# Copying the stacked query and key rows of a differential-attention head with six DMAs in place of twelve

## The chip, the cores and the metric

The kernel runs on one core of one Trainium2 chip. The metric is device time in microseconds (us) of one execution; lower is better. Three runs of the kernel before took 710.76, 712.08 and 713.83 us, so the median is 712.08 us.

## The reference

Two decoder layers for 512 tokens of width 1024. Layer 0 joins a gated MLP (A), a differential attention of 8 heads (B) and a cross-attention to 256 memory tokens (M); layer 1 joins a convolution, a sparse attention and another cross-attention. Each layer ends in an output projection and a residual sum. The change lies in B of layer 0:

```python
def diff_attention(q, k, v, lam):
    ...
        s = jnp.einsum('bhmqd,bhmkd->bhmqk', qi, k).astype(jnp.float32) * scale
        s = jnp.where(kpos[None, :] <= qpos[:, None], s, -jnp.inf)
        p = jax.nn.softmax(s, axis=-1)
        pd = p[:, :, 0] - lam * p[:, :, 1]
        return jnp.einsum('bhqk,bhkd->bhqd', pd.astype(v.dtype), v)
```

Each head has two maps (m = 0 and 1) with queries and keys of 32 numbers. The difference of the two softmaxes is multiplied with the values.

## The kernel before, in words

Numbers are held as a high part and a low part (high = the rounded number, low = what the rounding left), and a product is the sum of three TensorE products: high by high, high by low, low by high (`mm3`, L402 to L404). Weights come from DRAM in units of 128x1024 (`load_unit`, DMA at L384); ScalarE makes the high part (L386) and GpSimd the low part (L389).

`b_qk(c)`, c = 0 to 3, projects the queries and keys of two heads (L872, products at L402 to L404), normalizes and rotates them on VectorE (L879 to L887), transposes them on TensorE (L399) and writes high parts `th` (ScalarE, L376) and low parts `tl` (VectorE, L377). In each, index j = 0 is queries and j = 1 keys; rows are the dimensions, columns the 512 tokens.

`b_stack(c, h)` then puts the three products of a head's scores into one: it copies rows of 32 partitions so that 96 partitions hold, for the queries, high, low, high, and for the keys, high, high, low. One matmul over 96 rows then gives the whole score. The copies are DMAs from SBUF to SBUF, issued by SyncE (SP) at L904: 2 maps x 2 sides x 3 row groups = 12 of 32x512 for each head, 96 for the 8 heads.

`b_attn` (L941) goes through the 8 heads. For each it takes the four blocks of 128 queries from the last to the first: `causal_scores` multiplies (L927) and masks (VectorE, L929), ScalarE takes exponentials (L958), VectorE joins the maps (L959 to L962), TensorE transposes (L399 through `transposed`), ScalarE copies (L938), and TensorE multiplies by the values (L965). After a head's first block, the stack of the next head is asked for (L969), so the copies have the rest of the head to arrive. Only the first stack is asked for right before its use (L943).

The work of B is merged with a list of fillers (L1014 to L1016): the projections `b_qk(2)`, `b_qk(3)`, gates, the rest of A, memory keys and values. Then `m_attn` (L590, scores at L601 and L602, exponentials at L607, values at L586 to L588) is merged with the first part of the output projection (`out_part`, L638; products at L402 to L404).

The order of the instructions on each engine isn't the order of the code. `tile.TileContext(nc, schedule_with_timeline_sim=True)` (L1383) orders them at build time by a simulated timeline and adds the waits. Each engine then runs its own list in order. So a change of some DMAs may move instructions on every engine.

SBUF is handed out in pages by `Arena`: the class "x" has pages of 2048 words, and a request of 1024 words cuts one in two.

Of the kernel before, what the change touches and what calls it, by code (L numbers as in the profile page):

```python
# [24 lines left out]
F32R = mybir.dt.float32r  # L25
# [6 lines left out]
P = 128  # L32
S = 512
# [252 lines left out]
def emit(ctx, tc, nc, D, out):  # L286
# [8 lines left out]
    def SC():  # L295
        return Scope(arenas)
# [9 lines left out]
    dma = nc.sync.dma_start  # L306
    act = A.activation

    def f32(t):
        return t.bitcast(F32)  # L310

    def bc(ap, shape):
        return ap.broadcast_to(list(shape))

    def tok(i):
        return slice(i * P, (i + 1) * P)
# [51 lines left out]
    def rstd(sc, ss, scale, n, eps=EPS, parts=P):  # L368
        v = sc([P, n])[:parts]
        G.tensor_scalar(v, ss, scale, eps, MUL, ADD)  # L370
        r = sc([P, n])[:parts]
        G.tensor_tensor(r, v, mhalf[:parts, :n], ALU.pow)  # L372
        return r

    def split(src, h, l, eng=None):
        act(h, src, AF.Copy)  # L376
        (eng or V).tensor_tensor(l, src, f32(h), SUB)  # L377
# [20 lines left out]
    def tr(o, i, k=P):  # L398
        nc.tensor.transpose(o, i, ident[:k, :k])  # L399
# [45 lines left out]
    def proj_N(hs, units, order, n, loaded=()):  # L445


        order = list(order)
        per = S // n
        groups = [order[a:a + per] for a in range(0, len(order), per)]  # L450
        psc = [SC() for _ in groups]
        ps = [c.ps("d", [P, per, n]) for c in psc]
        k0 = 0
        for m, part in enumerate(units):
            with (loaded[m][0] if m < len(loaded) else SC()) as wsc:
                w = loaded[m][1] if m < len(loaded) else unit_parts(wsc, part, n)
                for a, g in enumerate(groups):
                    for b, i in enumerate(g):
                        for j, (wh, wl) in enumerate(w):
                            k = k0 + j  # L460
                            mm3(ps[a][:, b, :], hs[0][k // 4][:, k % 4, tok(i)], hs[1][k // 4][:, k % 4, tok(i)],
                                wh, wl, k + b == 0, k == KT - 1 and b == len(g) - 1)
                    if k0 + len(w) == KT:
                        for b, i in enumerate(g):
                            yield i, ps[a][:, b, :]
                        psc[a].close()
                k0 += len(w)

    def halves(name):
        i, n = UIDX[name]  # L470
        u = [(KT // n, D["wall"][i + j]) for j in range(n)]
        return [u[:n // 2], u[n // 2:]]
# [393 lines left out]
    bst = {}  # L866

    def b_qk(c):

        tsc = SC()  # L870
        th, tl = tsc([P, 2, S], F32R), tsc([P, 2, S], F32R)
        for i, p in proj_N(h0, halves(f"bqk{c}"), range(NT), 256):  # L872
            with SC() as sc:
                t = sc([P, 2, 4, 32])
                t3 = t.rearrange("p j m d -> p (j m) d")
                tf = t.rearrange("p j m d -> p (j m d)")
                act(tf, p, AF.Square)
                ss = sc([P, 8])
                V.tensor_reduce(ss, t3, AX.X, ADD)  # L879
                r = rstd(sc, ss, 1.0 / 32, 8)  # L880
                p4 = p.rearrange("p (j m d) -> p j m d", j=2, d=32)
                u = sc([P, 2, 4, 8])
                V.tensor_tensor(u, p4[:, :, :, 0:8], bc(bsg[:, i, :, :].unsqueeze(2), [P, 2, 4, 8]), MUL)
                V.tensor_tensor(p4, p4, bc(bcg[:, i, :, :].unsqueeze(2), [P, 2, 4, 32]), MUL)
                V.tensor_tensor(p4[:, :, :, 0:4], p4[:, :, :, 0:4], u[:, :, :, 4:8], ADD)
                V.tensor_tensor(p4[:, :, :, 4:8], p4[:, :, :, 4:8], u[:, :, :, 0:4], ADD)
                V.tensor_tensor(t3, p.rearrange("p (j d) -> p j d", d=32), bc(r.unsqueeze(2), [P, 8, 32]), MUL)  # L887
                pt = sc.ps("t", [P, 2, P])
                for k in range(2):
                    tr(pt[:, k, :], tf[:, k * P:(k + 1) * P])  # L890
                split(pt, th[:, :, tok(i)], tl[:, :, tok(i)])
            yield UT / 2 + 220
        bst[c] = (th, tl, tsc)

    def b_stack(c, h):

        th, tl, tsc = bst[c]
        sc = SC()
        st = sc([96, 4, S], F32R)
        for m in range(2):  # L900
            r0 = 64 * h + 32 * m
            for j, srcs in ((1, (th, th, tl)), (0, (th, tl, th))):
                for r, s in enumerate(srcs):
                    dma(f32(st[32 * r:32 * r + 32, 2 * j + m, :]), f32(s[r0:r0 + 32, j, :]))  # L904
        if h == 1:
            tsc.close()
        return st[:, 0:2, :], st[:, 2:4, :], sc
# [33 lines left out]
    def b_attn(order):  # L941
        heads = [(c, g, h) for c in range(2) for g in range(2) for h in range(2)]
        nxt = b_stack(0, 0)  # L943
        for n, (c, g, h) in enumerate(heads):
            ft = 2 * c + g
# [8 lines left out]
            for a, i in enumerate(order):  # L954
                with SC() as sc:
                    e, nm = causal_scores(sc, i, [[(qs[:, m, tok(i)], ks[:, m, :])] for m in range(2)])
                    for m in range(2):
                        act(e[m], e[m], AF.Exp, bias=nm[:, m:m + 1], scale=-1.0, accum_out=l[:, i, m:m + 1])  # L958
                    V.reciprocal(rl[:, i, :], l[:, i, :])  # L959
                    cf = sc([P, 1])  # L960
                    V.scalar_tensor_tensor(cf, l[:, i, 0:1], nlam, rl[:, i, 1:2], MUL, MUL)
                    V.scalar_tensor_tensor(e[1], e[1], cf, e[0], MUL, ADD)  # L962
                    pe = transposed(sc, e[1], i)
                    for k in range(i + 1):
                        mm(o[:, i, :], pe[:, k, :], bV[k // 2][:, k % 2, hc:hc + 64], start=k == 0, stop=k == i)  # L965
                if a == 0 and n + 1 < len(heads):
                    c2, g2, h2 = heads[n + 1]
                    yield from until(lambda: 2 * c2 + g2 in bst)
                    nxt = b_stack(2 * c2 + g2, h2)  # L969
                yield (i + 1) * 430  # L970
# [39 lines left out]
    for c in range(2):  # L1010
        drain(b_qk(c))
    banks(*P_L0)
    move("w", "x", W_DENSE - W_ATTN)
    fill = seq(b_qk(2), b_qk(3), gates_T(h0, [f"bg{f}" for f in range(4)], [yB[a][:, b, :] for a, b in pair]), a_gates(),  # L1014
               mem_prep(), m_q0(), m_gate0(), call(hsc.close), mem_kv(0), mem_kv(1), call(mem_sc.close))
    drain(merge((b_attn(rev), 1.0), (fill, FILL0)))  # L1016
# [328 lines left out]
    srcs = [(yD[0], 4, 2), (yD[1], 6, 2)]  # L1345
# [47 lines left out]
```

## Time and profile before

| | |
|---|---|
| median of 3 runs | 712.08 us (710.76 to 713.83) |
| the profiled execution, its own time | 711.15 us |
| its span in the trace | 709.4 us |
| mean granted TensorE clock | 0.988 of full |
| TensorE (PE) busy | 668.7 us, 94% of the span |
| VectorE (DVE), ScalarE (ACT), GpSimd (POOL) busy | 495.0, 377.8, 391.0 us |
| chain that ended last | PE 70%, DVE 12%, POOL 7%, ACT 4%, DMA 3%, issue 3%, SPq 0% |
| copies of the stacks | 96 DMAs of 64 KB, issued from 89.2 to 199.5 us |

How to read it: the profiled execution is 0.93 us below the median, and 1.75 us of it lie outside the span. PE busy is the time in which a matmul is under way. PE and the weight loads (PEld) run side by side. PEclk is the granted TensorE clock: 1.00 is the upper of its two levels (2.4 GHz), 0.50 the lower (1.2 GHz). SPq is SyncE's queue, which issues all DMAs of this kernel; the time that it takes to issue one is not counted as busy.

### The profile page before, as it was taken

The page shows a single profiled execution, that of the slowest core. Times are in us where ns is not written, and L with a number is a line of the kernel's source. Part 1 is how long each engine was busy: PE and PEld are TensorE (multiplying, and loading weights), DVE is VectorE, ACT ScalarE, POOL GpSimd, SP SyncE. Part 2 cuts the span into 40 slices and gives each one's busy share as a digit, 9 for nine tenths or more (in the row PEclk, how much of TensorE's full clock was granted, in tenths as well). Part 3 has the DMA queues.
Part 4 walks back from the last instruction along what each step waited for, and adds up shares of the span by engine and source line. Part 5 has one row for each costly group of instructions (what it writes and reads, how often), then busy time and mean ns, then how long its engine had stood idle before and what let it go on. Part 6 is the DMA issues. An engine that isn't in the chain of part 4 may idle for free.

```text
span 709.4 us, 11064 instructions
## 1 busy us (share of the span) xinstructions
PE 668.7 (94%) x3819; PEld 567.5 (80%) x3819; DVE 495.0 (70%) x1204; ACT 377.8 (53%) x846; POOL 391.0 (55%) x414
## 2 busy tenths in 40 slices
PE   4999989999999997799999999989999999999997
PEld 3789989888888875688888888768677888788875
DVE  4606668667666865786274979979777877998773
ACT  5345345556455676563353576632445656675541
POOL 3367877475436767442564779956664523421650
PEclk9999999999999999899999999989999999999999
DMA  8532134464313254222232411104021101120121
GB/s 301 185 118 91 60 90 142 136 177 127 107 56 121 88 197 135 85 66 84 65 105 75 148 63 58 61 0 149 31 89 60 61 30 60 42 79 1 61 75 74
DMA packets 22376, 66.56 MB, mean 94 GB/s; under 512 B 3504, under 2 KB 3760, under 8 KB 22320
## 3 DMA queue, kind: packets, MB, share of 16 engines
q1 hardware_dynamic: 22320, 65.86, 28.6%
q8 instruction: 30, 0.49, 0.3%
q14 instruction: 26, 0.21, 0.1%
HBM read 57.46 MB, written 2.10 MB: 84 GB/s over the span
## 4 chain that ended last, share of the span: by engine, by line
PE 70%; DVE 12%; POOL 7%; ACT 4%; DMA 3%; issue 3%; SPq 0%; POOLq 0%; ACTq 0%; DVEq 0%
PE banks L403 17%; PE banks L404 17%; PE banks L402 17%; PE banks L399 5%; PE banks L927 4%; POOL arena_r L389 4%; DMA arena_f<-in_wall_dram 3%; POOL arena_f L372 3%; DVE arena_r L377 2%; PE banks L1212 2%; PE banks L965 2%; ACT arena_r L386 1%; DVE arena_f L929 1%; PE banks L1182 1%; DVE banks L1261 1%
## 5 line engine op out<-in xcount | busy, mean ns | idle before, releaser
L389 POOL TENSOR_TENSOR arena_r<-arena_f,arena_r 128x512 fp32r<-128x512 f32 (+1 forms) x174 | 227.7, 1334 | 183.5 <-ACT arena_r L386 175.4
L402 PE MATMUL banks<-arena_r 128*128 128x512 f32 (+2 forms) x784 | 291.8, 376 | 5.9 <-ACT arena_r L386 1.9
L403 PE MATMUL banks<-arena_r 128*128 128x512 f32 (+2 forms) x784 | 292.2, 373 | 2.2 <-POOL arena_r L389 1.4
L404 PE MATMUL banks<-arena_r 128*128 128x512 f32 (+2 forms) x784 | 290.7, 373 | 0.0
L402 PEld LDWEIGHTS banks<-arena_r 128*128 128x128 f32 x784 | 150.0, 192 | 31.4 <-ACT arena_r L386 3.2
L403 PEld LDWEIGHTS banks<-arena_r 128*128 128x128 f32 x784 | 150.3, 192 | 26.0 <-POOL arena_r L389 2.7
L404 PEld LDWEIGHTS banks<-arena_r 128*128 128x128 f32 x784 | 149.9, 191 | 22.3 <-DVE arena_r L377 0.3
L386 ACT ACTIVATE arena_r<-arena_f 128x1024 fp32r<-128x1024 f32 (+2 forms) x87 | 91.1, 1049 | 67.2 <-issue 19.7
L399 PE MATMUL banks<-const,arena_f 128*128 128x128 f32 (+1 forms) x507 | 81.9, 279 | 13.9 <-DVE arena_f L417 9.4
L929 DVE CUSTOM_DVE_ANT_0 arena_f<-banks,const 128x512 f32<-128x512 f32 (+3 forms) x128 | 60.4, 484 | 35.0 <-PE banks L927 28.5
L376 ACT ACTIVATE arena_r<-banks 128x512 fp32r<-128x512 f32 (+1 forms) x112 | 57.7, 532 | 46.3 <-PE banks L399 32.7
L377 DVE TENSOR_TENSOR arena_r<-banks,arena_r 128x512 fp32r<-128x512 f32 (+1 forms) x112 | 66.7, 608 | 22.2 <-ACT arena_r L376 21.6
L399 PEld LDWEIGHTS banks<-const,arena_f 128*128 128x128 f32 (+1 forms) x507 | 61.9, 144 | 25.1 <-DVE arena_f L417 9.9
L372 POOL TENSOR_TENSOR arena_f<-arena_f,const 128x4 f32<-128x4 f32 (+3 forms) x60 | 68.0, 1135 | 3.6
L1261 DVE SCALAR_TENSOR_TENSOR banks<-arena_f,const,banks 128x482 f32<-128x482 f32 (+14 forms) x90 | 66.1, 734 | 1.4
L927 PE MATMUL banks<-arena_r 128*128 128x512 f32 (+7 forms) x192 | 50.8, 339 | 4.4 <-DVE arena_f L929 2.1
L958 ACT ACTIVATE arena_f<-arena_f 128x512 f32<-128x512 f32 (+3 forms) x64 | 35.8, 562 | 26.6 <-DVE arena_f L929 26.2
L1189 ACT ACTIVATE arena_f<-arena_f 128x256 f32<-128x256 f32 (+3 forms) x64 | 35.6, 559 | 26.0 <-DVE arena_f L929 25.2
L657 DVE TENSOR_TENSOR arena_f<-arena_f,banks 128x512 f32<-128x512 f32 x40 | 27.0, 684 | 26.6 <-PE banks L404 26.0
L574 POOL TENSOR_SCALAR arena_f<-arena_f 128x512 f32<-128x512 f32 (+3 forms) x32 | 19.9, 626 | 39.6 <-DVE arena_f L1191 33.7
L927 PEld LDWEIGHTS banks<-arena_r 128*128 128x128 f32 (+1 forms) x192 | 32.8, 190 | 10.6 <-DVE arena_f L929 4.6
L1259 POOL TENSOR_TENSOR arena_f<-arena_f 128x482 f32<-128x482 f32 (+29 forms) x30 | 37.8, 1259 | 2.9 <-DVE arena_f L608 0.9
(177 smaller groups left out, 809.8 us busy)
## 6 DMA issues: line engine op xcount, KB each, us to landing
arena_f<-in_wall_dram SPq DMA_DIRECT2D x88, 512.0 KB, 3.3
arena_r<-arena_r SPq DMA_DIRECT2D x96, 64.0 KB, 2.0
arena_f<-in_x_dram SPq DMA_DIRECT2D x7, 512.0 KB, 6.0
arena_f<-in_w_dram SPq DMA_DIRECT2D x4, 512.0 KB, 3.8
out_dram<-arena_f SPq DMA_DIRECT2D x8, 256.0 KB, 2.0
arena_f<-in_norms_dram SPq DMA_DIRECT2D x3, 512.0 KB, 4.3
arena_f<-in_mem_dram SPq DMA_DIRECT2D x2, 512.0 KB, 3.2
arena_f<-in_wqb_dram SPq DMA_DIRECT2D x2, 420.0 KB, 3.2
```

The costliest lines, as they stand in the source:

```text
L372: G.tensor_tensor(r, v, mhalf[:parts, :n], ALU.pow)
L376: act(h, src, AF.Copy)
L377: (eng or V).tensor_tensor(l, src, f32(h), SUB)
L386: act(h, raw, AF.Copy)
L389: G.tensor_tensor(l[:, c], raw[:, c], f32(h[:, c]), SUB)
L399: nc.tensor.transpose(o, i, ident[:k, :k])
L402: mm(o, lh, rh, start=first, stop=False)
L403: mm(o, lh, rl, start=False, stop=False)
L404: mm(o, ll, rh, start=False, stop=last)
L927: mm(t[:, a % per, :], q, k[:, :w], start=b == 0, stop=b == len(qk) - 1)
L929: V.tensor_tensor_reduce(e[a], t[:, a % per, :], cmask[:, S - w:], -1.0, -NEG, ADD, ALU.min, nm[:, a:a + 1])
L1261: V.scalar_tensor_tensor(acc[:, z:], hc[:, :S - z], cw[:, f, k:k + 1], acc[:, z:], MUL, ADD)
```

## The change

High and low parts of queries and keys lie in one tile `tt` of four planes: query high, query low, key high, key low. `th` and `tl` are now views of it with a step of two planes. A copy takes a query plane and a key plane at once: two runs of 512 words for each of 32 partitions, at a step of 2, 1 or 3 planes in the source and 2 in the target. So a head's stack is 2 maps x 3 row groups = 6 DMAs of 32x2x512, 48 for the 8 heads. What is computed, and what is stored in the stack, stay the same.

```diff
     def b_qk(c):
 
         tsc = SC()
-        th, tl = tsc([P, 2, S], F32R), tsc([P, 2, S], F32R)
+        tt = tsc([P, 4, S], F32R)
+        th, tl = tt[:, 0::2, :], tt[:, 1::2, :]
...
-        bst[c] = (th, tl, tsc)
+        bst[c] = (tt, tsc)
 
     def b_stack(c, h):
 
-        th, tl, tsc = bst[c]
+        tt, tsc = bst[c]
         sc = SC()
         st = sc([96, 4, S], F32R)
         for m in range(2):
             r0 = 64 * h + 32 * m
-            for j, srcs in ((1, (th, th, tl)), (0, (th, tl, th))):
-                for r, s in enumerate(srcs):
-                    dma(f32(st[32 * r:32 * r + 32, 2 * j + m, :]), f32(s[r0:r0 + 32, j, :]))
+            for r, (q, k) in enumerate(((0, 2), (1, 2), (0, 3))):
+                dma(f32(st[32 * r:32 * r + 32, m::2, :]), f32(tt[r0:r0 + 32, q:k + 1:k - q, :]))
```

The scheduler's order changes with it. The lines of `b_qk` from L872 on are one higher in the changed file, L904 and what follows keep their numbers. Three places:

The DMA list of SyncE from the first stack on, before (-) and now (+); L904 are the copies of the stacks, L384 the weight units, L839 and L843 two constants of A.

```order
-L904 DMA arena_r<-arena_r 32x512 x24
+L904 DMA arena_r<-arena_r 32x2x512 x12
+L384 DMA arena_f<-in_wall_dram 128x1024 x4
+L904 DMA arena_r<-arena_r 32x2x512 x18
+L384 DMA arena_f<-in_wall_dram 128x1024 x4
+L904 DMA arena_r<-arena_r 32x2x512 x9
+L839 DMA arena_f<-in_wsT_dram 128x512
+L904 DMA arena_r<-arena_r 32x2x512 x3
 L384 DMA arena_f<-in_wall_dram 128x1024 x3
-L904 DMA arena_r<-arena_r 32x512 x36
```

The first two stacks still stand together at the head of the list, and the next three behind one more group of weight loads; four such loads stand between them where there were three.

TensorE at the first head's first scores. L399 x2 are transposes of `b_qk(1)`, L402 to L404 the products of `b_qk(2)`, L927 the scores: 512 columns for the last block of queries, 384 for the one before it. Before:

```order
L404 MATMUL banks<-arena_r 128x256
L399 MATMUL banks<-const,arena_f 128x128 x2
L927 MATMUL banks<-arena_r 128x512
L399 MATMUL banks<-const,arena_f 128x128 x2
L402 MATMUL banks<-arena_r 128x256
L403 MATMUL banks<-arena_r 128x256
```

Now:

```order
L404 MATMUL banks<-arena_r 128x256
L399 MATMUL banks<-const,arena_f 128x128 x2
L927 MATMUL banks<-arena_r 128x512 x2
L927 MATMUL banks<-arena_r 128x384
L399 MATMUL banks<-const,arena_f 128x128 x2
L402 MATMUL banks<-arena_r 128x256
```

The second map's scores of the last block stood 46 products, four more transposes and one 384-column score further down; they now follow the first map's at once, with a score of the next block behind them, ahead of all products of `b_qk(2)`.

TensorE at the start of `m_attn`, before (-) and now (+): L601 and L602 are its scores, L399 x4 the transposes of its exponentials, L402 and L403 products of the output projection.

```order
 L601 MATMUL banks<-arena_r 128x256
 L602 MATMUL banks<-arena_r 128x256
+L399 MATMUL banks<-const,arena_f 128x128 x4
 L601 MATMUL banks<-arena_r 128x256
 L602 MATMUL banks<-arena_r 128x256
 L601 MATMUL banks<-arena_r 128x256
 L602 MATMUL banks<-arena_r 128x256
-L402 MATMUL banks<-arena_r 128x512
-L403 MATMUL banks<-arena_r 128x512
```

Twelve products of the output projection stood behind the scores; four transposes now stand among the scores, and the products come later. So the cross-attention runs further ahead of the output projection: behind its last product with the values (L588) there follow 142 products of the output projection before the next transposes, where there were 125.

## Rows read from the trace of the kernel before

**Rows 1.** The page: busy engines, chain that ended last.
```profile
span 709.4 us, 11064 instructions
PE 668.7 (94%) x3819; PEld 567.5 (80%) x3819; DVE 495.0 (70%) x1204; ACT 377.8 (53%) x846; POOL 391.0 (55%) x414
...
PE 70%; DVE 12%; POOL 7%; ACT 4%; DMA 3%; issue 3%; SPq 0%; POOLq 0%; ACTq 0%; DVEq 0%
```

**Rows 2.** Busy time by stretch: stretch, PE, PEld, DVE, ACT, POOL, PEclk, DMA share, GB/s.
```profile
92.00:95.00 3.00, 0.88 (x6) 0.52 (x5) 1.87 (x7) 0.66 (x2) 2.92 (x3) 0.95 0.40 98
95.00:260.00 165.00, 162.18 (x979) 143.04 (x978) 113.25 (x332) 96.03 (x235) 98.56 (x110) 0.99 0.41 123
260.00:300.00 40.00, 29.70 (x154) 23.80 (x153) 28.13 (x64) 24.18 (x62) 24.96 (x31) 0.91 0.39 129
300.00:345.00 45.00, 45.00 (x292) 38.50 (x291) 26.74 (x49) 21.95 (x44) 15.97 (x13) 1.00 0.19 59
```

**Rows 3.** Timeline of PE at the first head: start, duration, what, [idle before, releaser].
```profile
92.04 0.38 PE L399 MATMUL banks<-const,arena_f 128*128 128x128 f32 x2
94.53 0.63 PE L927 MATMUL banks<-arena_r 96*128 96x512 f32 x1 [2.12 <-DMA arena_r<-arena_r]
94.96 0.63 PE L399 MATMUL banks<-const,arena_f 128*128 128x128 f32 x2
95.24 0.56 PE L402 MATMUL banks<-arena_r 128*128 128x256 f32 x1
...
99.57 0.34 PE L927 MATMUL banks<-arena_r 96*128 96x384 f32 x1
99.75 0.28 PE L403 MATMUL banks<-arena_r 128*128 128x256 f32 x1
...
102.47 0.40 PE L927 MATMUL banks<-arena_r 96*128 96x512 f32 x1
102.70 0.28 PE L403 MATMUL banks<-arena_r 128*128 128x256 f32 x1
```

**Rows 4.** SP's copies at L904: 89 to 91, 91.7 to 93 us, whole span; landings.
```profile
L904 SPq DMA_DIRECT2D arena_r<-arena_r x3: 579/588/593, 89.2 to 90.5; - x3
L904 SPq DMA_DIRECT2D arena_r<-arena_r x3: 588/589/592, 91.7 to 93.0; - x3
L904 SPq DMA_DIRECT2D arena_r<-arena_r x96: 507/588/1386, 89.2 to 199.5; - x96
DMA to landing us min/median/max: 1.9/2.0/5.0
```

**Rows 5.** SP's weight units at L384, whole span: issue in ns, min/median/max.
```profile
L384 SPq DMA_DIRECT2D arena_f<-in_wall_dram x88: 327/328/1132, 2.2 to 675.1; - x88
```

**Rows 6.** Waits of SP's queue: total us, times, longest.
```profile
SPq L384 <- ACT arena_r L386: 276.0, 41, 27.3
```

**Rows 7.** SP's list, by order of time.
```profile
89.20 15.72 SPq L904 DMA_DIRECT2D arena_r<-arena_r  x24
105.44 3.68 SPq L384 DMA_DIRECT2D arena_f<-in_wall_dram  x3
```

**Rows 8.** Busy time by stretch, one and two us each.
```profile
91.00:92.00 1.00, 1.00 (x10) 1.00 (x10) 0.58 (x3) 0.00 (x0) 0.84 (x3) 1.00 0.52 127
97.00:98.00 1.00, 1.00 (x7) 1.00 (x7) 0.42 (x1) 0.00 (x0) 0.43 (x1) 0.50 0.12 25
98.00:99.00 1.00, 1.00 (x10) 1.00 (x10) 0.00 (x0) 0.00 (x0) 0.00 (x0) 0.95 0.49 121
```

**Rows 9.** Timeline of ACT: a store of adjacent runs, one at a step.
```profile
95.63 0.38 ACT L376 ACTIVATE arena_r<-banks 128x256 fp32r<-128x256 f32 x1 [2.67 <-PE banks L399]
258.65 0.38 ACT L535 ACTIVATE arena_r<-banks 64x256 fp32r<-64x256 f32 x1
```

**Rows 10.** Timeline of PE at the start of the cross-attention.
```profile
283.59 0.50 PE L601 MATMUL banks<-arena_r 128*128 128x256 f32 x2 [2.98 <-ACT arena_r L376]
288.84 0.58 PE L601 MATMUL banks<-arena_r 128*128 128x256 f32 x1 [3.54 <-ACT arena_f L610]
293.23 0.40 PE L402 MATMUL banks<-arena_r 128*128 128x512 f32 x1
293.47 0.39 PE L403 MATMUL banks<-arena_r 128*128 128x512 f32 x1
```

## The prediction

> **What bounds the kernel now.** I read the page first, then the busy time by stretch, then the timeline of TensorE (PE) and the list of SyncE (SP) where the copies of the stacks run. The reader is to see that PE is the bound: it is busy for 668.7 of 709.4 us, the chain that ended last runs for 70% of the span over PE, and SP's queue has 0% of it [rows 1]. So only PE's idle time, 40.7 us in all, and its time at the lower clock can be won.
>
> By stretch [rows 2]: from 92 to 95 us, at the first head's first scores, PE has 2.12 us of idle time; from 95 to 260 us, where all other stacks are copied and used, 165 - 162.18 = 2.82 us; from 260 to 300 us, where attention B ends and the cross-attention begins, 10.30 us; from 300 to 345 us none. The copies end at 199.5 us [rows 4].
>
> The 2.12 us are the one place where PE waits for a stack: the first score starts at 94.53, released by a copy [rows 3]. The price of that stop is more than the wait. PE had run at the upper clock; after the stop the granted clock is 0.50 until about 98.1 us (0.50 from 97 to 98, 0.95 from 98 to 99) [rows 8]. That is some 3.5 us at half speed, or 1.75 us of work lost.
>
> **The change, part by part.**
>
> *Half as many copies.* A copy takes SP 588 ns to issue [rows 4], and with the gap behind it 0.62 us (the third starts at 90.5 and three starts lie between 91.7 and 93.0, so four steps take 2.5 us). 48 fewer save at most 48 x 0.62 = 29.8 us of SP's time. I cost this at nothing, since what SP gets free is waiting time: SP waits 276.0 us for ScalarE to give back weight buffers [rows 6]. From 95 to 260 us only 2.82 us of PE's time are idle, so this is the most that earlier weights could give there. The stacks of heads 1 to 7 are hidden by a head's length: the first 24 copies are issued by 104.92 us [rows 7], and PE loses nothing to them. If that cover went, each late stack would cost a stop like the first.
>
> The Trainium skill says in "DMA: Bandwidth & Descriptors", section "Rules for kernel authors", that many small transfers should be coalesced, since under 64 KB one pays mostly overhead. By that rule the change gains; the rows here put the overhead on a queue that waits anyway, and no row shows PE waiting for a second stack.
>
> *Twice the bytes in each.* The bytes stay, and so do the 2 KB runs. While only copies ran, the DMA share was 0.52 at one copy per 0.62 us [rows 8]: one copy keeps the 16 DMA engines busy for 0.52 x 0.62 = 0.32 us. A double one needs 0.64, so I take its landing at 2.0 [rows 4] + 0.32 = 2.32 us. Engines would then be nearly full while twelve copies follow each other.
>
> The same page of the Trainium skill, section "Anatomy of one DMA — SWDGE (gpsimd) path", fits a DMA by 2.0 us and bytes at 436 GB/s, for another issuing path than this one. An estimate from it is 0.15 us for 64 KB more, and the sum below would be 0.17 us lower.
>
> *What one new copy costs SP.* No row has a copy with two runs for each partition. The low end is a weight unit's 328 ns [rows 5], the high end twice the copy's 588 ns, if the time counts rows (64 in place of 32). I take 588 ns: the nearest row is the same copy, and the larger weight unit with its four times as many partitions is the cheaper one, so rows alone don't set the price.
>
> *The first head.* Now PE's list has both maps' scores and a 384-column score of the next block in front of everything else, so PE waits for six copies, as before, but these six are the whole stack. Before, the sixth copy started at 90.5 + 3 x 0.62 = 92.36, landed 2.0 later, and PE started 0.17 us behind that. Now the sixth starts at the same time and lands at 94.68; the second map's score starts at 94.85. The three matmuls at the lower clock need about 0.43 us for the 512-column score (94.53 to 94.96 [rows 3]), 0.32 for 384 columns by the same rate, and 0.28 for two transposes (94.96 to 95.24). The products then start at 95.88 in place of 95.24: +0.64. The two moved scores are saved later, at the upper clock: 0.23 (102.47 to 102.70) and 0.18 (99.57 to 99.75), so -0.41 [rows 3]. The first map's score, alone, can run up to 1.2 us earlier and falls into the wait. **Net +0.23 us.** VectorE waits in order too: the masking of the second map now stands ahead of the last low parts of `b_qk(1)`. They are wanted for head 2's stack, behind the next weight loads, so I cost that at nothing.
>
> With 328 ns per copy, the sixth starts at 90.5 + 3 x 0.36 = 91.58 and PE is 0.78 us earlier: -0.55. With 1.18 us (1.21 with the gap) the third copy starts at 91.62 and the sixth at 95.25; PE starts at 97.74, and the net is +3.1 us.
>
> *Strided stores.* High and low parts are now written with a step of two planes between their two runs. A store of two adjacent runs takes ScalarE 0.38 us, and one with a step (L535) also 0.38 [rows 9]. Cost nothing, and ScalarE is busy 377.8 us only [rows 1]. The page of 2048 words was cut in two and is now taken whole, so no other page becomes scarce.
>
> *The new order elsewhere.* The scheduler moved work among the fillers from 95 to 345 us. What it moved is the same work, on a PE that is full from 95 to 260 and from 300 to 345 us. Its idle time there, 2.82 us, can go up or down by about itself. From 260 to 300 us the two longest waits are 2.98 us for the memory keys and 3.54 us for the softmax that frees a score bank [rows 10]. The transposes that now stand there wait for the same softmax. I take zero.
>
> **Sum.** 711.15 (the profiled execution) + 0.23 = 711.4. The median of the runs is 0.93 above that execution, so a run would show 712.3 us. What a measurement of this kernel can tell from no change is 0.5%, or 3.56 us: faster is below 708.5, slower above 715.6.
>
> **The rivals.**
>
> *Faster: SP's queue holds the early part back.* With the queue emptier, the first stop becomes so short that the clock isn't lowered (-1.75 - 2.12), and weights come early enough to take the 2.82 us. That gives 712.1 - 6.7 = 705.4, and with the first stop alone 708.2. For it: the first wait does end on a copy [rows 3]. Against it: the wait needs a low issue cost, and SP waits for buffers far more than it issues [rows 6]. Chance 0.17.
>
> *Slower: the issue time counts rows.* Place: the first stack; price +3.1, or 715.2 us at 1.18 us per copy. It passes 3.56 us from about 1.26 us per copy on. For it: before, the copy of 32 rows already costs more than a weight unit. Against it: the 128 rows of a weight unit cost less [rows 4, 5]. Chance 0.07.
>
> *Slower: the cross-attention loses its cover.* Seventeen products fewer stand among its matmuls (142 in place of 125 come behind), at 0.23 us (293.23 to 293.47 [rows 10]) 3.9 us of work. Where the softmax chain is longer than what stands between, PE stops, as it does for 3.54 us at 288.84 [rows 10]; a stop of that kind also costs half speed for some 3.5 us, 1.75 us more. All of it: 712.1 + 3.9 + 1.7 = 717.7 us. It decides as soon as the chain of a score pair outlasts the work behind it. Against it: PE is full for 45 us from 300 us on, with VectorE at 26.74 and ScalarE at 21.95 [rows 2], so the chain had room. Chance 0.16.
>
> *It doesn't do what it says:* engine time and bytes of the copies stay, so on a full DMA system nothing would be won at all; this ends like the forecast and is counted with it.
>
> **How the numbers follow.** The forecast, 712.3 with its own range 709 to 715.3, has 0.60; the rivals 0.17, 0.07 and 0.16. Nearly all of the first rival and 0.02 of the forecast's lower tail are faster: 0.19. Slower are 0.15 of the third, 0.03 of the second and 0.02 of the forecast: 0.20. The rest, 0.61, is the same. The range reaches from the lower half of the first rival, 706.5, to the end of the third, 717.5.
>
> **What would show it.** Right: 48 copies at about 0.6 us each, landing at 2.2 to 2.5 us; the second map's first score near 94.9 us; PE idle under 4 us from 95 to 260 us and about 10 from 260 to 300. Wrong: copies at over 1 us, PE waiting for a stack past 96 us; no stretch at 0.50 clock after the first stack; PE waits for ScalarE or VectorE between 300 and 345 us, where there were none.

## The result and the profile after

Twelve runs of the changed kernel have a median of 719.3 us (714.27 to 721.37), twelve of the kernel before 711.73 us. The ratio is **1.0103, 95% interval 1.0085 to 1.0122: slower by 1%**, 7.6 us by the medians. The profiled execution took 721.37 us, 10.2 us more than the one before; it is the longest of the twelve, so its trace holds more loss than the medians do.

The page of the changed kernel, to be held against [rows 1]; its last line is the group of the copies, with the size of one and the median time from issue to landing:

```profile
span 719.6 us, 11008 instructions
...
PE 675.9 (94%) x3819; PEld 572.5 (80%) x3819; DVE 495.8 (69%) x1204; ACT 378.1 (53%) x846; POOL 389.4 (54%) x414
...
PE 69%; DVE 11%; POOL 8%; DMA 5%; ACT 4%; issue 3%; SPq 1%; POOLq 0%; ACTq 0%; DVEq 0%
...
arena_r<-arena_r SPq DMA_DIRECT2D x48, 128.0 KB, 2.4
```

PE does the same 3819 matmuls and is busy 7.2 us longer: the same work at a lower clock (0.974 on average, before 0.988). Its idle time grew by 3.0 us. The copies themselves came as forecast, landing after 2.4 us. SP's issues of them (count, ns min/median/max, first and last start), as [rows 4]:

```profile
L904 SPq DMA_DIRECT2D arena_r<-arena_r x48: 585/593/1578, 89.6 to 206.4; - x48
```

By stretch, changed kernel, columns as in [rows 2]:

```profile
92.00:95.00 3.00, 1.27 (x8) 0.72 (x6) 1.71 (x5) 0.66 (x2) 2.84 (x4) 1.00 0.88 202
95.00:260.00 165.00, 159.87 (x945) 141.57 (x946) 110.62 (x324) 90.93 (x222) 90.78 (x105) 0.96 0.39 117
260.00:300.00 40.00, 29.75 (x150) 23.33 (x149) 26.77 (x63) 25.79 (x64) 30.99 (x36) 0.84 0.42 145
300.00:345.00 45.00, 45.00 (x285) 38.45 (x286) 29.02 (x56) 22.41 (x54) 13.18 (x10) 0.95 0.18 60
```

The first head isn't where it went. From 95 to 260 us PE's idle time went from 2.82 to 5.13 us, and the clock from 0.99 to 0.96; from 260 to 300 us the idle time stayed (10.25 against 10.30) and the clock fell from 0.91 to 0.84. PE's timeline at its longer waits, first head, then the two stops that are new, then the cross-attention (as [rows 3, 10]):

```profile
93.98 0.49 PE L927 MATMUL banks<-arena_r 96*128 96x512 f32 x1 [1.21 <-DMA arena_r<-arena_r]
95.26 0.64 PE L927 MATMUL banks<-arena_r 96*128 96x512 f32 x2 [0.79 <-DMA arena_r<-arena_r]
...
161.43 1.16 PE L856 MATMUL banks<-arena_f 128*128 128x128 f32 x8 [0.86 <-POOL arena_f L840]
...
166.05 1.11 PE L399 MATMUL banks<-const,arena_f 128*128 128x128 f32 x4 [2.29 <-DVE arena_f L980]
...
289.71 0.51 PE L601 MATMUL banks<-arena_r 128*128 128x256 f32 x2 [1.47 <-ACT arena_r L376]
...
293.98 1.11 PE L399 MATMUL banks<-const,arena_f 128*128 128x128 f32 x4 [2.32 <-DVE arena_f L980]
296.98 0.58 PE L601 MATMUL banks<-arena_r 128*128 128x256 f32 x1 [1.89 <-ACT arena_f L610]
```

**Stretch A, 160 to 176 us.** Busy time and clock in steps of two us, changed kernel:

```profile
160.00:162.00 2.00, 1.14 (x9) 0.82 (x8) 0.70 (x2) 1.85 (x4) 1.09 (x4) 1.00 0.91 232
162.00:164.00 2.00, 1.10 (x8) 0.70 (x6) 0.56 (x2) 0.53 (x2) 2.00 (x2) 1.00 0.97 373
164.00:166.00 2.00, 0.00 (x0) 0.00 (x0) 0.42 (x1) 0.18 (x2) 1.53 (x3) 0.67 0.21 84
166.00:168.00 2.00, 1.95 (x10) 1.96 (x10) 0.80 (x2) 0.00 (x0) 0.00 (x0) 0.50 0.75 260
...
172.00:174.00 2.00, 2.00 (x10) 1.90 (x10) 1.69 (x7) 1.78 (x5) 0.00 (x0) 0.50 0.00 0
174.00:176.00 2.00, 2.00 (x9) 1.61 (x8) 0.98 (x4) 0.68 (x3) 1.29 (x1) 0.77 0.02 4
```

In these 16 us PE is busy for 11.93 us (4.07 idle), and at the granted clock that is 7.6 us of full-speed work: 8.4 us are lost, half to idling, half to the clock. In the kernel before the same 16 us hold 15.3 us of work, all at 1.00. What PE waits for is on the list of POOL, in the changed kernel:

```profile
158.48 0.19 POOL L976 TENSOR_TENSOR arena_f<-arena_f 128x4 f32<-128x4 f32 x1
160.74 0.64 POOL L840 TENSOR_SCALAR_AFFINE_SELECT arena_f<-arena_f 128x512 f32<-128x512 f32 x1 [2.06 <-DMA arena_f<-in_wsT_dram]
...
162.89 2.49 POOL L389 TENSOR_TENSOR arena_r<-arena_f,arena_r 128x512 fp32r<-128x512 f32 x2
165.33 0.20 POOL L979 TENSOR_TENSOR arena_f<-arena_f 128x4 f32<-128x4 f32 x1
```

L976 to L979 are the norm at a head's end, for which L980 and PE's transposes wait. The masking of A's weights (L840) stands inside this chain and waits for its load; so do two low parts of a weight (L389). The load goes out behind nine copies on SP's list, which take 11.31 us, 3.1 of them a wait until PE (L927) gives a stack's page back:

```profile
146.17 11.31 SPq L904 DMA_DIRECT2D arena_r<-arena_r  x9
157.59 0.52 SPq L839 DMA_DIRECT2D arena_f<-in_wsT_dram  x1
```

Before, the same load went out at 151.34, ahead of thirteen of the copies, and L840 waited 0.40 us:

```profile
149.35 0.19 POOL L976 TENSOR_TENSOR arena_f<-arena_f 128x4 f32<-128x4 f32 x1
...
151.15 2.54 POOL L389 TENSOR_TENSOR arena_r<-arena_f,arena_r 128x512 fp32r<-128x512 f32 x2 [1.04 <-ACT arena_r L386]
153.65 1.00 POOL L372 TENSOR_TENSOR arena_f<-arena_f,const 128x4 f32<-128x4 f32 x1
155.06 0.64 POOL L840 TENSOR_SCALAR_AFFINE_SELECT arena_f<-arena_f 128x512 f32<-128x512 f32 x1 [0.40 <-DMA arena_f<-in_wsT_dram]
155.67 0.20 POOL L979 TENSOR_TENSOR arena_f<-arena_f 128x4 f32<-128x4 f32 x1
```

So the chain of the kernel before has the same mask and two low parts in it, and on POOL it took 6.5 us (149.35 to 155.87), in the changed kernel 7.05. What changed more is PE's own work beside it. Busy time from the start of the sum ahead of the chain (L974 on VectorE) to the start of the transposes behind it, before and in the changed kernel, columns as in [rows 2]:

```profile
148.49:158.82 10.33, 10.33 (x51) 8.52 (x50) 5.91 (x22) 6.16 (x15) 8.28 (x11) 1.00 0.53 157
156.45:166.05 9.60, 5.79 (x31) 4.44 (x30) 4.29 (x16) 4.44 (x11) 6.85 (x10) 0.93 0.68 205
```

Before, PE had 51 matmuls there, 10.33 us of work, and didn't stop. Now it has 31, 5.79 us, and stands idle for 3.81 us. A chain with waiters in it and a list of PE that no longer covers it come together here.

Where the loss arises can be read at five places up to which PE has done the same matmuls in both kernels, only in another order. PE starts the next one, in us:

| matmuls done | before | changed | behind by |
|---|---|---|---|
| 477 (first head) | 94.96 | 95.26 | 0.30 |
| 699 | 125.64 | 126.12 | 0.48 |
| 917 | 165.88 | 173.09 | 7.21 |
| 1397 | 249.00 | 255.03 | 6.03 |
| 1913 (behind the cross-attention) | 348.81 | 358.74 | 9.93 |

So 6.7 us arise from matmul 700 to 917, the stretch around A (40.2 us before, 47.0 now), and 3.9 us from 1398 to 1913, around the cross-attention (99.8 and 103.7 us). Behind it hardly anything more is lost (10.2 us at the end).

### The profile page after: what moved, and what is told of

It is laid out like the page before. It is cut to its first block, busy times and chain, and to the rows that moved or that the text cites. A ratio compares the mean times of both kernels' runs of the same rounds, so it can differ in the third digit from the quotient of the medians.

```text
span 719.6 us, 11008 instructions
## 1 busy us (share of the span) xinstructions
PE 675.9 (94%) x3819; PEld 572.5 (80%) x3819; DVE 495.8 (69%) x1204; ACT 378.1 (53%) x846; POOL 389.4 (54%) x414
## 4 chain that ended last, share of the span: by engine, by line
PE 69%; DVE 11%; POOL 8%; DMA 5%; ACT 4%; issue 3%; SPq 1%; POOLq 0%; ACTq 0%; DVEq 0%
PE banks L403 17%; PE banks L402 17%; PE banks L404 17%; PE banks L399 6%; DMA arena_f<-in_wall_dram 4%; PE banks L927 3%; POOL arena_f L372 3%; POOL arena_r L389 3%; PE banks L1212 2%; DVE arena_r L377 2%; PE banks L965 2%; PE banks L1088 1%; ACT arena_r L386 1%; PE banks L1182 1%; DVE arena_f L929 1%
## 5 line engine op out<-in xcount | busy, mean ns | idle before, releaser
L389 POOL TENSOR_TENSOR arena_r<-arena_f,arena_r 128x512 fp32r<-128x512 f32 (+1 forms) x174 | 226.0, 1325 | 180.2 <-ACT arena_r L386 172.4
L402 PE MATMUL banks<-arena_r 128*128 128x512 f32 (+2 forms) x784 | 292.3, 377 | 5.9 <-DVE arena_f L582 3.2
L403 PE MATMUL banks<-arena_r 128*128 128x512 f32 (+2 forms) x784 | 292.8, 374 | 2.6 <-POOL arena_r L389 1.5
L404 PE MATMUL banks<-arena_r 128*128 128x512 f32 (+2 forms) x784 | 291.1, 373 | 0.0
L402 PEld LDWEIGHTS banks<-arena_r 128*128 128x128 f32 x784 | 150.4, 192 | 32.0 <-DVE arena_f L582 3.6
L403 PEld LDWEIGHTS banks<-arena_r 128*128 128x128 f32 x784 | 150.8, 192 | 27.0 <-POOL arena_r L389 2.8
L404 PEld LDWEIGHTS banks<-arena_r 128*128 128x128 f32 x784 | 150.5, 192 | 22.8 <-DVE arena_r L377 0.3
L399 PE MATMUL banks<-const,arena_f 128*128 128x128 f32 (+1 forms) x507 | 83.3, 283 | 19.5 <-DVE arena_f L417 10.0
L399 PEld LDWEIGHTS banks<-const,arena_f 128*128 128x128 f32 (+1 forms) x507 | 62.3, 146 | 30.4 <-DVE arena_f L417 10.4
L929 DVE CUSTOM_DVE_ANT_0 arena_f<-banks,const 128x384 f32<-128x384 f32 (+3 forms) x128 | 60.7, 485 | 28.5 <-PE banks L927 22.5
L372 POOL TENSOR_TENSOR arena_f<-arena_f,const 128x4 f32<-128x4 f32 (+3 forms) x60 | 68.0, 1135 | 3.7
L927 PE MATMUL banks<-arena_r 128*128 128x512 f32 (+7 forms) x192 | 50.1, 338 | 3.8 <-DMA arena_r<-arena_r 2.0
L927 PEld LDWEIGHTS banks<-arena_r 128*128 128x128 f32 (+1 forms) x192 | 32.8, 191 | 9.8 <-DVE arena_f L929 3.7
```

The lines of the kernel that those rows point to most:

```text
L389: G.tensor_tensor(l[:, c], raw[:, c], f32(h[:, c]), SUB)
L402: mm(o, lh, rh, start=first, stop=False)
L403: mm(o, lh, rl, start=False, stop=False)
L404: mm(o, ll, rh, start=False, stop=last)
L927: mm(t[:, a % per, :], q, k[:, :w], start=b == 0, stop=b == len(qk) - 1)
L929: V.tensor_tensor_reduce(e[a], t[:, a % per, :], cmask[:, S - w:], -1.0, -NEG, ADD, ALU.min, nm[:, a:a + 1])
```

## The experiments

**Order theory:** the copies are neutral; the time went into the order that the scheduler made of the rest, above all in stretch A. **Copy theory:** the 128 KB copies, or the page with its strided stores, are slow or late themselves. A third question is stretch B, the cross-attention from 285 to 305 us.

To part the copies from the order, the kernels below build the program twice. The first build tells the place of each instruction; the second adds, between neighbours on one engine, an edge that fixes their sequence and adds no wait:

```python
for lane in lanes.values():            # one list per engine
    lane.sort(key=lambda i: key[i.name])
    for a, b in zip(lane, lane[1:]):
        tc.add_manual_dep(b, a.name, NoSync)
```

### Which of the two: copies or order

`e1`, `e2`: only what stands in `key` and the form of the copies differ. The edits of the pinned kernels are shortened.

```diff
 # e1
-nc = build(shapes)
+_, order = program(shapes, pairs=False)      # twelve copies
+nc, _ = program(shapes, True, order)         # six copies in that order
 # e2
+_, order = program(shapes, pairs=True)       # six copies
+nc, _ = program(shapes, False, order)        # twelve copies in that order
```

> Six two-run copies per stack, with every instruction of PE, DVE, ACT and POOL pinned to the order that they have in the kernel before, and on SP each copy at the place of the first of the two that it replaces. Order theory (the copies cost nothing, the changed kernel loses by the new order of the other instructions): the time of the kernel before, 711.7 us, between 709 and 714; the affine_select waits for its mask no more than before (0.4 us) and PE's half clock lies at 285 to 293 us as before. Copy theory (the copies of 128 KB or their strided stores are what costs): near the changed kernel, 717 to 721 us.

> Twelve one-run copies per stack from the one page, with every instruction of PE, DVE, ACT and POOL pinned to the order of the changed kernel, and on SP each pair of copies at the place of the one that stood for them. Order theory: near the changed kernel, 716 to 722 us, with the affine_select's wait and the half clock after it at about 165 us; it may be 1 or 2 us more, as twelve issues of 0.59 us stand where six stood ahead of the mask's load. Copy theory: the time of the kernel before, 709 to 714 us.

`e3`: the new page with the old copies.

```diff
-            for r, (q, k) in enumerate(((0, 2), (1, 2), (0, 3))):
-                dma(f32(st[32 * r:32 * r + 32, m::2, :]), f32(tt[r0:r0 + 32, q:k + 1:k - q, :]))
+            for j, srcs in ((1, (2, 2, 3)), (0, (0, 1, 0))):
+                for r, s in enumerate(srcs):
+                    dma(f32(st[32 * r:32 * r + 32, 2 * j + m, :]), f32(tt[r0:r0 + 32, s, :]))
```

> The one page with its halves in the new order, but twelve copies of one run as before; the instructions then fall into the order of the kernel before by themselves. If the page's layout or the strided stores into it cost anything, the time is over 713 us; all theories that look to the copies or to the order expect 711.7 us, between 709.5 and 713.

| | copies | order | median us | ratio to before, 95% |
|---|---|---|---|---|
| changed kernel | 6 | new | 719.3 | 1.0103 (1.0085 to 1.0122) |
| e1 | 6 | old | 711.52 | 1.0003 (0.9982 to 1.0024) |
| e2 | 12 | new | 727.57 | 1.0248 (1.0213 to 1.0284) |
| e3, new page | 12 | old | 712.64 | 1.0024 (0.9995 to 1.0052) |

This decides between the two theories. With the old order six copies are as fast as twelve; with the new order both forms are slower. e1 by stretch, clock back at 0.91 from 260 to 300 us:

```profile
95.00:260.00 165.00, 161.28 (x978) 141.52 (x977) 115.50 (x333) 97.07 (x236) 101.04 (x111) 1.00 0.40 123
260.00:300.00 40.00, 30.50 (x160) 24.80 (x161) 27.05 (x64) 24.35 (x62) 23.29 (x30) 0.91 0.33 119
```

e2 missed the order theory's upper end by 5.6 us, in a way that adds to it. Where the mask's load stands behind the copies, each copy saved counts. In e2's SP list nine copies are eighteen, the first 24 take 16.76 us, and the load goes out 8.7 us later than with six:

```profile
88.61 16.76 SPq L904 DMA_DIRECT2D arena_r<-arena_r  x24
...
166.25 0.58 SPq L839 DMA_DIRECT2D arena_f<-in_wsT_dram  x1
```

PE then waits 3.26 us for L840 at 169.86. Of e2's distance to the changed kernel its profile shows 2.4 us at the first head (matmul 477 done at 97.64 us) and 5.7 in the stretch around A. So the saved issues are worth nothing in the old order and 8 us (medians) to 10 us (ratios) in the new one. No run pins the new order with six copies and moves nothing. That pinning itself costs nothing is shown by e1 for the old order, and for the new one by PE's work ahead of the moves: from matmul 478 to 699 it takes 30.86 us in the changed kernel, 30.87 and 30.84 in e4 and e12 below, which are pinned.

### Where in the order: stretch A

There are places at which both orders have done the same instructions on every engine, among them those with 699, 917 and 1397 matmuls done. The next three kernels (six copies, pinned) change from one order to the other there; A means the stretch from 700 to 917.

```diff
 key[i] = (part, (old, new)[NEW[part]][i])    # parts: to A, A, between, B to the end
+NEW = [0, 1, 0, 0]     # e9:  new order in A alone
+NEW = [0, 0, 0, 1]     # e10: new order from B on alone
+NEW = [1, 0, 1, 1]     # e11: old order in A alone
```

> Six copies. Between two places at which both orders have done the same instructions on every engine, the program follows the changed kernel's order: on PE from its 691st to its 884th matmul or transpose, which holds the affine_select, the first products with the masked weights and the wait at 166 us. Everything ahead of it and behind it follows the order of the kernel before. If the order in this stretch costs what the profiles show up to 268 us (6.0 us), then 717.5 us, between 716 and 719.5. If the loss is spread over the whole program, or comes from how the stretch is reached: 711.5 to 715 us.

> Six copies in the order of the kernel before up to the 1360th instruction of PE (about 250 us), and from there to the end in the changed kernel's order, which holds the start of the cross-attention and the half clock at 291 to 305 us. If this stretch costs by its own order what the profiles show there (some 4 us): 715.5 us, between 714 and 717.5. If the loss there only follows from how late it is reached: 710 to 713 us.

> The changed kernel's order everywhere but in the stretch with the affine_select (PE's 691st to 884th instruction), which follows the order of the kernel before. If the two stretches add up: the changed kernel less 6 us, 713.3 us, between 712 and 715.5. If the stretch's loss comes back as another wait behind it: 716 to 720 us.

| | new order in | median us | ratio to before, 95% |
|---|---|---|---|
| e9 | A | 721.66 | 1.0171 (1.0144 to 1.0199) |
| e10 | B and behind | 711.45 | 1.0015 (0.9998 to 1.0032) |
| e11 | all but A | 713.31 | 1.0043 (1.0026 to 1.0060) |

Stretch A alone is enough for the whole loss, also when its stop at the joint (below) is taken off. Without it (e11) the median came out at the expected 713.3 us, 6.0 below the changed kernel; by the ratios, which allow for the kernel before being 1.2 us faster beside e11, the loss falls from 1.03% to 0.43%, by 4.3 us. Stretch B costs 1.1 us by its own order (0.15%, at most 0.32%, and its interval also holds none). The profiles agree: from matmul 1398 to 1913 e10 takes 100.8 us, and e2, e4 and e12, with the same order there, 100.2, 100.9 and 100.2, against 99.8 before. The changed kernel's profile has 103.7, so most of its 3.9 us there belong to that one execution. A's 6.7 us and some 1 us of B are about the 7.6 us by the medians. e9 overshot: 12.2 us by its ratio in place of 6. Its timeline of PE names a part of it: beside the two known stops it has one at the joint that neither order has.

```profile
126.25 0.50 PE L402 MATMUL banks<-arena_r 128*128 128x512 f32 x1 [2.29 <-DVE arena_f L888]
...
163.36 1.16 PE L856 MATMUL banks<-arena_f 128*128 128x128 f32 x8 [0.98 <-POOL arena_f L840]
167.97 1.11 PE L399 MATMUL banks<-const,arena_f 128*128 128x128 f32 x4 [2.29 <-DVE arena_f L980]
```

The stop at the joint takes 2.29 us and some 1.6 us of clock behind it, so about 8 us are left for A itself. That putting A in costs 8 us and taking it out gives back 4 to 6 says that the parts don't simply add up; why is not shown. In the profile e11 takes 40.4 us for A, as little as the kernel before.

### What in stretch A: the chain on POOL and the load ahead of it

Here the changed kernel's own order is pinned, and single instructions are moved.

```diff
 # e4: SP, the mask's load ahead of the nine copies
+key[mask_load] = key[first_of_the_nine] - 0.5
 # e12: e4, and one head's norm chain in one piece
+for n, i in enumerate(chain):  key[i] = key[chain[0]] + 0.1 * n
 # e5: e4, and the chains of all heads
+for chain in chains:
+    for n, i in enumerate(chain):  key[i] = key[chain[0]] + 0.1 * n
 # e6: e5, and on ACT one conversion (L386) behind the exponentials
+key[conversion] = key[first_L610] + 0.5
```

> The changed kernel with its own order pinned on all engines, and one instruction moved: on SP the load of the mask's weights (line 839) stands ahead of the nine copies that it stood behind. Order theory: the affine_select (line 840) no longer waits 2.06 us, PE's wait for the norm (line 980) near 166 us shrinks by about 2 us and the half clock after it shortens; 714 to 718 us. Copy theory: no change, 719 us, since that stop is then not what costs.

> The changed kernel in its own order, with the mask's load moved ahead of the nine copies, and of one head alone, the one at the affine_select, the norm chain on POOL in one piece (lines 976, 977, 370, 372, 979 in a row, the affine_select and one weight's low parts behind them). The other heads' chains stay as they are, unlike the run in which all were moved. If the stop at 164 us is what is left of the loss in that stretch: 2 to 4 us below the run with the mask's load alone (716.15 us), so 712 to 714.5 us. If the wait only moves on to the products behind the affine_select: 715 to 717 us.

> The changed kernel with its own order pinned, the mask's load moved as in the run before, and one thing more: on POOL, of each head's norm chain (lines 976, 977, 370, 372, 979) the last four follow directly on the first, so that no low part of a weight (line 389, two of 2.49 us together) and no affine_select stands within a chain. Order theory: PE's wait of 2.14 us for line 980 at 163.8 us goes, and with it most of the half clock up to 173 us (some 3 us more); near 291 us the wait for line 980 goes too, but there the exponentials (line 607) come last next, so that little is gained; 710 to 714 us. If the half clock there doesn't hang on this wait: 713.5 to 716 us. Copy theory: no change from the run before.

> The run before with one more move: on ACT the conversion of a weight (line 386) that waits for its load stands behind the first four exponentials of the cross-attention and the scaling of their result (lines 607, 610) rather than ahead of them. Order theory: about 1 to 3 us below the run before, as PE's wait near 291 us and the half clock after it shorten; 708 to 713 us. If the late weight is wanted by PE just as soon, its matmuls wait instead, and nothing changes.

| | median us | ratio to before, 95% | stretch A, us |
|---|---|---|---|
| changed kernel | 719.3 | 1.0103 (1.0085 to 1.0122) | 47.0 |
| e4 | 716.15 | 1.0077 (1.0046 to 1.0108) | 45.7 |
| e12 | 714.79 | 1.0060 (1.0037 to 1.0083) | 43.4 |
| e5 | 716.91 | 1.0084 (1.0059 to 1.0109) | 43.0 |
| e6 | 719.04 | 1.0100 (1.0076 to 1.0124) | 43.5 |

The last column is PE's time from matmul 700 to 917 in the profiled execution; the kernel before took 40.2 us.

e4 alone isn't parted from the changed kernel by the intervals; in stretch A it gains 1.3 us. Its mask load went out only 2.1 us earlier (155.53): in SP's waits it now stands itself for 9.8 us on L927 and 1.8 us on L962, which free its page. Then L840 waited 0.61 us, but PE still waited 2.14 us for L980 at 163.82: the two low parts of a weight stood in the chain. e12 takes them out too, and its interval lies clear below the changed kernel's. PE's waits in e12:

```profile
160.40 1.16 PE L856 MATMUL banks<-arena_f 128*128 128x128 f32 x8 [0.83 <-POOL arena_f L840]
162.40 0.33 PE L927 MATMUL banks<-arena_r 96*128 96x128 f32 x1 [0.66 <-DVE arena_f L929]
...
166.12 1.67 PE L965 MATMUL banks<-arena_f 128*128 128x64 f32 x10 [0.84 <-ACT arena_f L938]
```

The long stop is gone, and little of the half clock is left (columns as in stretch A's table):

```profile
166.00:168.00 2.00, 1.88 (x12) 1.88 (x13) 1.97 (x5) 0.99 (x3) 0.00 (x0) 0.74 0.94 304
168.00:170.00 2.00, 2.00 (x9) 1.62 (x8) 1.71 (x7) 1.95 (x6) 0.00 (x0) 0.50 0.87 301
170.00:172.00 2.00, 2.00 (x9) 1.64 (x8) 0.87 (x3) 0.60 (x2) 1.29 (x1) 0.91 0.90 352
```

So two moved details give back 0.43 of the 1.03% (3 us; 4.5 by the medians), and in stretch A 3.6 of the 6.7 us. By its median e12 came just over its expected 712 to 714.5 us; but the kernel before was faster beside it (710.56 us), and by the ratios e12 is only 1.2 us below e4, not the expected 2 to 4, and the two aren't parted by their intervals.

e5 and e6 missed. e5 does in all heads what e12 does in one and gains nothing over e4 (the intervals of e4, e5 and e12 overlap). Its profile shows that A isn't the reason: there it takes 43.0 us, as little as e12. The moves in the other heads cost it again behind A: from matmul 918 to 1397 it takes 84.8 us, where e12 takes 82.1, and from 1398 to 1913 103.2, where e12 takes 100.2. In e6 PE's wait for L610 fell from e5's 1.78 us to 0.57, but the conversion that was moved back now holds up POOL, where a norm of the memory keys (L372) stands behind that weight's low parts; L517 waits for it, and PE for L517:

```profile
296.62 1.11 PE L399 MATMUL banks<-const,arena_f 128*128 128x128 f32 x4 [2.86 <-DVE arena_f L517]
```

### Other orders

`e7`, not pinned: the loops over the copies swapped. `e8`: e1 with three moves in stretch B.

```diff
 # e7
-        for m in range(2):
-            r0 = 64 * h + 32 * m
-            for r, (q, k) in enumerate(((0, 2), (1, 2), (0, 3))):
+        for r, (q, k) in enumerate(((0, 2), (1, 2), (0, 3))):
+            for m in range(2):
+                r0 = 64 * h + 32 * m
 # e8
+key[conversion_L386] = key[next_L376] + 0.25
+key[first two L604] = key[first_L504] - 0.5 ...
+key[six products L402 to L404] = key[ninth_score] - 0.5 ...
```

> The changed kernel with the two loops over its six copies swapped (row group outside, map inside): the same six copies in another sequence, and no order pinned, so that the instructions fall into a third order. Order theory: the time can be anything from about 708 to 722 us and differs from the changed kernel's by more than the copies could explain, with no stop at the affine_select or another one elsewhere. Copy theory: the changed kernel's time, 717 to 721 us, since the same bytes move in as many copies.

> Six copies in the order of the kernel before (the first of these runs), with three moves where PE stood idle for 2.98 and 3.54 us at 283.6 and 288.8 us: on ACT one high part (line 376) ahead of a weight's conversion (line 386) that waited for POOL; on DVE the first two maxima of the scores (line 604) ahead of four steps of the norm (lines 504, 507); on PE six matmuls of the output projection (lines 402 to 404) ahead of the scores that waited for line 610. If stops are what costs, order by order: PE's two waits shrink by 3 to 4 us in all and the half clock at 285 to 292 us shortens by 1 to 3 us; 705 to 709 us. If what is saved there comes back as another wait: 710 to 713 us.

e7 took 715.82 us, ratio 1.0074 (1.0047 to 1.0101). A third order, again slower than before, again with a stop at the mask (PE waits 2.13 us for L840 at 163.42) and, in that stretch, none for L980. By the medians it is 3.5 us below the changed kernel, though the intervals overlap; it fits the order theory, but doesn't decide anything by itself.

e8 took 710.75 us, ratio 0.9996 (0.9971 to 1.0022): nothing gained. Of the two waits of 2.98 and 3.54 us [rows 10] it made one:

```profile
289.24 0.80 PE L402 MATMUL banks<-arena_r 128*128 128x512 f32 x1 [6.34 <-DVE arena_f L517]
```

The products that were moved up need a bank that L517 on DVE has yet to read, and in e8 that waits for POOL:

```profile
288.50 0.69 DVE L517 TENSOR_TENSOR arena_f<-banks,arena_f 128x512 f32<-128x512 f32 x1 [1.24 <-POOL arena_f L372]
```

No version here beats the kernel before by more than its interval.

## Why the prediction was wrong

**Where it failed:** the step "The new order elsewhere", with its "I take zero". It took PE's idle time from 95 to 260 us as the whole stake ("can go up or down by about itself"). The idle time did go up by no more than that, from 2.82 to 5.13 us, though past the 4 us that the prediction gave as its sign. But the new stops also cost clock, and the step that priced this, at 1.75 us, did so for the first head and, in a rival, for the cross-attention, not here. In stretch A the clock cost 4.3 us more, and the stretch 6.7 us in all. That PE "is full" there was no reason for zero: it was full because its list had 10.33 us of work beside the norm chain, and the new list has 5.79. The order shown ahead of the prediction had one part of it in sight: the SP list with nine copies now ahead of L839. I looked there at the copies and not at what is queued behind them. PE's and POOL's lists at that place are not among the orders shown there.

**Point by point.** *Half as many copies, cost nothing:* right in the old order (e1, 1.0003). The reason given, that SP waits anyway, holds only while nothing urgent stands behind a copy; in the new order twelve copies cost 8 to 10 us more than six (e2). *Twice the bytes:* 2.32 us to landing forecast, 2.4 measured. *What one new copy costs SP:* 588 ns taken, 593 measured; the rival that counts rows is out. The low branch, at 328 ns, was added up wrongly: it leaves the first two steps at the old price (90.5 + 3 x 0.36), where the high branch changes them too. By the same working the sixth copy would start at 89.2 + 5 x 0.36 = 91.0, not 91.58; the measured price made that branch idle. *The first head:* PE waits 1.21 + 0.79 = 2.00 us in place of 2.12, and the second map's score starts at 95.26, forecast 94.85; too small to matter. *Strided stores:* cost nothing, as taken (e3's interval holds 1; at most 0.52%).

**The rivals.** The faster one, SP's queue holding the early part back, isn't borne out by the time: e1 frees the queue and gains nothing. Its first part does show in e1's profile, though. There the stop at the first head is two short ones, and the clock stays at 1.00 behind them:

```profile
93.13 0.47 PE L927 MATMUL banks<-arena_r 96*128 96x512 f32 x1 [0.62 <-DMA arena_r<-arena_r]
94.58 0.41 PE L399 MATMUL banks<-const,arena_f 128*128 128x128 f32 x2 [0.97 <-DVE banks L886]
```

That profile is 1.8 us ahead of the kernel before up to matmul 1913 (347.00 against 348.81 us) and has lost it by matmul 3000 (559.71 against 559.37), with half clock from 498.9 to 502.3 us, where the kernel before has none. The slower one at the cross-attention had the right mechanism (a chain without cover, then half speed) at the wrong place: stops appeared there, but e10 prices that stretch's order at 1.1 us. Its 717.7 us was near the result by luck.

**What stays open:** of the 3 us by which e11 is still slower than the kernel before, B's order holds 1.1 by e10 (2.2 in e11's own profile, 102.0 against 99.8 us from matmul 1398 to 1913), and no run names the place of the rest. And e12 shows that the waits in the POOL chain are about half of stretch A, 3.6 of 6.7 us; what is left there are three waits under one us with half clock behind them. No run gives PE its old list in A and POOL its new one, so the shorter cover and the chain aren't parted from each other.

## What to carry to other kernels

Where a scheduler orders the program by a simulated timeline, an edit of the transfers is two edits: pin the old order and time the new transfers in it, then time the order by itself; here the first was worth nothing and the second 1%. In the new order look at each chain that TensorE waits for in two ways: how much of TensorE's own work stands beside it, before and after, and which early waiter stands in it or ahead of it (a load queued behind copies that wait for a page, a mask inside a norm). Moving the two that stood in the way paid (e12); moving all of their kind, or filling a gap with work whose bank isn't free, only moved the wait.

## What the runs showed of the hardware that was not expected

A copy with two runs of 2 KB for each of 32 partitions takes SP 593 ns to issue, the one with one run 588: for this shape the price lay in neither runs nor bytes. The Trainium skill's "DMA: Bandwidth & Descriptors", section "Rules for kernel authors", asks for coalescing small transfers. By that rule the change gains; e1 shows no gain where the queue has time, and the changed kernel gains 8 to 10 us on e2, where it has none.

The price of a stop isn't fixed. After the first head's wait of 2.12 us the clock was at 0.50 until about 98 us, worth 1.75 us [rows 8]; behind the waits of 160 to 166 us it stayed at 0.50 until about 175. In e12 it fell to 0.50 behind waits of which none was over 0.84 us. And much the same stop can go either way: at the first head e1 and e8 have one order, and PE waits 0.62 and 0.97 us in the one, 0.65 and 0.94 us in the other; the clock stayed at 1.00 in e1 and was 0.50 until about 98 us in e8.
